# A decoder layer in split fp32: the up projection's weights split by one instruction on each engine, and a table of biases as two products of narrow parts

## The chip, the cores and the metric

The kernel runs on one core of a Trainium2 chip. Its engines have names in the profile: PE multiplies matrices (PEld is its loading of weights), DVE and POOL work elementwise on vectors, ACT does activations, copies and casts, SP issues most loads; every engine takes its own instructions in the order in which they stand in its queue. The metric is the time of one execution on the device, in microseconds (us). The profile is of one such execution.

## The reference

One layer of a hybrid causal decoder on 256 tokens of 1024 features, all in float32. A combined projection feeds three attention mixers (top-64 sparse, dilated windows, blocks); a bias of each head from a table of 32 distance buckets is added to all logits; the mixers' outputs are gated, summed and projected. What follows is the part that the change's larger half lies in:

```python
bias_a = rel_bias[:, :A_HEADS]              # and bias_b, bias_c: columns of one (32, 24) table
logits = jnp.einsum('bqhd,bqkd->bqhk', qb, ksel) * scale + bias_tab[rel_bucket(dist)]
...
x = layer_norm(ALPHA * x + merged @ w_out[i], ln1_g[i], ln1_b[i])
h = jnp.square(jax.nn.relu(x @ w_up[i])) @ w_down[i]
ple = jax.nn.sigmoid(x @ w_ple_gate[i]) * (p[i] @ w_ple[i])
x = layer_norm(ALPHA * x + h + ple, ln2_g[i], ln2_b[i])
```

`w_up` is 1024 x 4096, `w_down` 4096 x 1024.

## The kernel before

**Products of parts.** PE multiplies in the type fp32r, which holds a narrower number than float32. So each operand is split into two parts, hi (the cast of the value) and lo (what the cast lost), and a product is three: hi by hi, hi by lo, lo by hi (`prod`, L183 to L191, matmul in L188). Weights arrive in units of 128 x 1024 or fewer columns (`Weights`, L79 to L139). For a unit, SP issues the load to a raw tile (L102), ACT casts raw to hi (L111, or L109 where the unit lies in an `Apart`), DVE subtracts hi from raw to get lo (L118, or L122 in an `Apart`), and for the first 58 units POOL does a share of the columns. `get` keeps this four units ahead of PE; raw, hi and lo have five buffers each.

**Blocks at listed places.** An `Apart` (L47 to L70) is a tile whose blocks of 128 columns lie at listed offsets. `runs` groups blocks that follow at equal steps; each run takes one instruction of ACT and one of DVE. In the 32 units of the up projection hi has its blocks at 16, 192, 320, ... and lo at 64, 208, 336, ...: the step from the first block to the second is larger than the others, so a run covers blocks 0 and 1 (128 x 256) and another the other six (128 x 768): two instructions on ACT (L109) and two on DVE (L122) per unit.

**The up projection** (L913 to L952). For each unit f, eight matmuls of 512 columns (L923: hi of the unit by both parts of x) and eight of 256 (L926: lo by the hi part of x) go to one PSUM bank. Then DVE adds the two halves (`tensor_reduce`, L907), ACT applies ReLU and square (L908, L909) and casts the result to the hi part of hT (L934), and DVE subtracts for its lo part (L935). Some units come in pairs whose results are combined for the Strassen-like down projection: then POOL forms four sums of the two (L945 to L948) and ACT (L951) and DVE (L952) split all seven blocks at once. Ahead of the down projection, its own operands are formed on DVE (`form`, L885 to L887) from rows of w_down that SP loads to tiles (wr, xr); xr takes the buffer of x1, which L923 and L926 read.

**The table of biases** (`bias_table`, L478 to L488). GpSimd's queue loads a one-hot matrix oh (36 x 384) and relt, the 32 x 24 table with four more rows (two loads, L482 and L483). PE multiplies the two in float32 (L485), ACT copies the 24 x 384 product to tab (L487), stores it to DRAM (L530), and SP reads it back as the tiles T (L265) that the mixers add (L461 and others). It happens between the first features: `feat` multiplies a block of the projection in one of three PSUM banks named mm, which are freed by the ACT cast and DVE subtraction of `k_pair` (L320), `q_pair` (L306, L307) or `v_out` (L400, L401).

**What sets the order.** The source is written once per step; the framework's scheduler lays the instructions of each engine out in a row by estimated times, except where the code pins them (`issue_after`, `keep_in_program_order`). So a change of an instruction's size can move others that it doesn't name.

Of the kernel before, what the change touches and what calls it, by code (L numbers as in the profile page):

```python
# [11 lines left out]
F32 = mybir.dt.float32  # L12
F32R = mybir.dt.float32r
ALU = mybir.AluOpType
# [11 lines left out]
N_BIAS = 24  # L26
# [5 lines left out]
N_U = 384  # L32
# [110 lines left out]
def hybrid_layer(ctx: ExitStack, tc: tile.TileContext, x0, xn, pT, wqk, wva, wvb, wg, wbc, wba,  # L143
                 wout, wup, wdn, wpg, wple, lnrow, rel, onehot, pick, out):
    nc = tc.nc
    pe, act, dve, pool = nc.tensor, nc.scalar, nc.vector, nc.gpsimd
# [55 lines left out]
    def inturn(t):  # L202
        return t.rearrange("p (a c) -> p c a", a=2)
# [28 lines left out]
    def add(*a, at=(0, 0), by=DV):  # L232
        i = n_u[0]
        n_u[0] += 1
        return W.add(*a, by=by if i < 58 else "v", at=at)
# [143 lines left out]
    op = pm.tile([128, 8, 2, S], F32R, name="op")  # L379
# [97 lines left out]

    def bias_table():  # L478
        relt = wk.tile([36, N_BIAS], F32, name="relt", tag="e")
        oh = wk.tile([36, N_U], F32, name="oh", tag="e")  # L480
        pool.dma_start(oh, onehot)
        pool.dma_start(relt[0:N_BUCKETS], rel)  # L482
        pool.dma_start(relt[N_BUCKETS:], pick)  # L483
        tab_ps = next(ps_v)
        pe.matmul(tab_ps[:N_BIAS, :N_U], lhsT=relt, rhs=oh, start=True, stop=True)  # L485
        tab = wk.tile([N_BIAS, N_U], F32, name="tab", tag="e")
        act.copy(tab, tab_ps[:N_BIAS, :N_U])  # L487
        return tab  # L488
# [3 lines left out]
    with ExitStack() as begin:  # L492
# [7 lines left out]
        with tc.high_priority(offset=1000):  # L500
            for k in range(KT):
                for i, (a, b) in enumerate(cut[k]):
                    e = nc.scalar if i else nc.sync
# [9 lines left out]
        for k in range(KT):  # L513
            for i, (w, x) in enumerate(((sh, xh), (sh, xl), (sl, xh))):
                for f in range(FIRST):
                    pe.matmul(pairs(first[f]), lhsT=w[:, k, 128 * f:128 * f + 128],  # L516
                              rhs=inturn(x[:, k]),
                              start=k == i == 0, stop=k == KT - 1 and i == 2)
        iq = [q_pair(ps, 0.125) for ps in first]
    tp, wk, wk2, sm = (right(n, b) for n, b in (("tp", 3), ("wk", 3), ("wk2", 2), ("sm", 6)))  # L520
    tab = bias_table()
    ps = feat(4)
    kI, kA = k_pair(ps[0:64], ps[0:64]), k_pair(ps[64:128], ps[64:128])
# [76 lines left out]
    for j in range(3):  # L600
        s = logits(kA, q)
        o = opair()
        for h in range(2):
# [4 lines left out]
            with tc.issue_after(W.subs[-3]):  # L608
                pool.tensor_tensor(ta[:, 0:128], natural(T, n % 3, 128, 256), am[:, 0:128],
                                   op=ALU.add)  # L610
                pool.tensor_tensor(ta[:, 128:384], natural(T, n % 3, 0, 256), am[:, 128:384],
                                   op=ALU.add)
# [17 lines left out]
    u_out += [add(wout[4 + i], 1024, wo[:, i, 0], wo[:, i, 1]) for i in range(4)]  # L630
    u_ple = [add(wple[i], 1024) for i in range(2)]
    u_pg = [add(wpg[i], 1024) for i in range(8)]
    UP = (16, *range(192, 1088, 128)), (64, *range(208, 1104, 128))
    u_up = [[add(wup[i], 1024, at=UP)] for i in range(32)]

    H = (slice(0, 512), slice(512, 1024))
# [219 lines left out]
    for k in (*SEQ, *LATE):  # L856
        i = PAIRS.index(k) if k in PAIRS else -1
# [39 lines left out]
    for k in (*SEQ, *LATE):  # L897
        if k in PAIRS:
            i = PAIRS.index(k)
# [13 lines left out]
    for f in range(32):  # L913
# [8 lines left out]
        for k, c in enumerate(cs):  # L922
            pe.matmul(ps, lhsT=hi[:, c], rhs=x1[:, :, k].rearrange("p b a t -> p a t b"),  # L923
                      start=k == 0, stop=False)
        for k, c in enumerate(cs):
            pe.matmul(ps[:, 0], lhsT=lo[:, c], rhs=x1[:, :, k, 0].rearrange("p b t -> p t b"),  # L926
                      start=False, stop=k == KT - 1)
# [239 lines left out]
```

## Time and profile before

| what | value |
|---|---|
| median of three runs (lowest, highest) | 417.76 us (416.52, 417.91) |
| the profiled execution | 417.77 us |
| its span, first to last instruction | 416.0 us |
| mean granted TensorE clock | 0.997 |
| PE busy | 405.4 us (97%) |
| DVE busy | 348.6 us (84%) |
| ACT busy | 277.4 us (67%) |
| POOL busy | 121.6 us (29%) |
| HBM read and written | 81.88 and 1.09 MB |

A row of a group of instructions reads: line, engine, operation, output<-inputs, shape and type, xcount | busy us, mean ns of one | idle us of the engine just before them, with what ended most of it. A row of a timeline reads: start, duration (of the whole group if xcount is over 1), engine, line, operation; in brackets the idle time before it and what released it. Durations overlap a little, since an engine starts an instruction before the last one's end is recorded; on PE the spacing of starts is the cost, not the length of one.

### The profile page before, as it was taken

The numbers are of one execution on the slowest core, as the hardware profiler recorded it, in microseconds if no ns is written. First come the engines' busy times: TensorE is split into PE (matmuls) and PEld (weight loads), VectorE is DVE, ScalarE is ACT, GpSimd is POOL, SyncE is SP. The second block draws the span as 40 slices with busy tenths as digits, with TensorE's granted clock in tenths as the row PEclk, the third lists the DMA queues.
The fourth block names the chain that finished last, engine by engine and source line by source line (L and its number), as shares of the span: only waits on it lengthen the run. The fifth ranks groups of instructions, "written<-read, shape, count | busy, mean of one in ns | idle before, by whom it ended". The sixth has DMA issues, their size and how long they took to land.

```text
span 416.0 us, 7828 instructions
## 1 busy us (share of the span) xinstructions
PE 405.4 (97%) x2804; PEld 374.4 (90%) x2804; DVE 348.6 (84%) x650; ACT 277.4 (67%) x530; POOL 121.6 (29%) x128
## 2 busy tenths in 40 slices
PE   8999999999999999999999999999999999999993
PEld 8989999999999999999887889999999988788883
DVE  4968669897777689889968889999999798999856
ACT  6877476495798786867515567887889766467310
POOL 1669456275353657500000002433430000000001
PEclk9999999999999999999999999999999999999998
DMA  8896766567464408478980686786576377556602
GB/s 288 298 327 188 267 165 201 169 201 258 148 204 135 134 9 290 125 218 260 335 310 12 219 284 198 227 288 197 189 215 199 102 277 231 185 167 207 198 2 102
DMA packets 27964, 83.49 MB, mean 201 GB/s; under 512 B 3184, under 2 KB 6792, under 8 KB 27540
## 3 DMA queue, kind: packets, MB, share of 16 engines
q1 hardware_dynamic: 27216, 80.46, 59.9%
q10 hardware_dynamic: 612, 2.46, 1.6%
q8 instruction: 22, 0.36, 0.4%
q14 instruction: 18, 0.15, 0.1%
q0 software_dynamic: 96, 0.06, 0.0%
HBM read 81.88 MB, written 1.09 MB: 199 GB/s over the span
## 4 chain that ended last, share of the span: by engine, by line
PE 82%; DVE 10%; DMA 3%; issue 3%; ACT 1%; POOL 0%; SPq 0%; DVEq 0%; ACTq 0%; POOLq 0%
PE mm L188 36%; PE b L188 16%; PE mm L923 13%; PE mm L926 7%; PE b L370 3%; DMA xr<-in_wdn_dram 3%; DVE wlo L118 3%; PE b L516 3%; PE b L412 1%; DVE wlo L122 1%; PE b L416 1%; ACT whi L111 1%; PE b L179 1%; DVE store L118 1%; DVE G L692 1%
## 5 line engine op out<-in xcount | busy, mean ns | idle before, releaser
L111 ACT CAST whi<-raw 128x1024 fp32r<-128x1024 f32 (+3 forms) x92 | 89.4, 986 | 35.4 <-PE b L188 14.6
L122 DVE TENSOR_TENSOR wlo<-raw,whi 128x256 fp32r<-128x256 f32 (+3 forms) x118 | 94.6, 825 | 16.1 <-ACT whi L111 13.2
L188 PE MATMUL mm<-xh,whi 128*128 128x256 f32 x336 | 89.1, 278 | 0.0
L122 POOL TENSOR_TENSOR wlo<-raw,whi 128x384 fp32r<-128x384 f32 (+1 forms) x50 | 68.6, 1382 | 65.2 <-ACT whi L111 58.6
L188 PE MATMUL mm<-xl,whi 128*128 128x256 f32 x336 | 87.1, 277 | 0.0
L188 PE MATMUL mm<-xh,wlo 128*128 128x256 f32 x336 | 79.4, 278 | 0.0
L188 PEld LDWEIGHTS mm<-xh,whi 128*128 128x128 f32 x336 | 64.4, 192 | 0.9
L188 PEld LDWEIGHTS mm<-xl,whi 128*128 128x128 f32 x336 | 64.5, 192 | 0.3
L923 PE MATMUL mm<-x,whi 128*128 128x512 f32 x256 | 60.7, 379 | 0.0
L188 PEld LDWEIGHTS mm<-xh,wlo 128*128 128x128 f32 x336 | 58.7, 192 | 0.2
L188 PE MATMUL b<-whi,store 128*128 128x512 f32 x168 | 52.6, 380 | 0.7 <-DVE store L698 0.4
L923 PEld LDWEIGHTS mm<-x,whi 128*128 128x128 f32 x256 | 46.1, 190 | 5.2
L118 DVE TENSOR_TENSOR wlo<-raw,whi 128x1024 fp32r<-128x1024 f32 (+2 forms) x38 | 43.3, 1162 | 3.3 <-ACT whi L111 3.1
L740 POOL TENSOR_TENSOR rs<-rs,half 128x1 f32<-128x1 f32 x4 | 2.2, 554 | 143.3 <-DVE rs L739 143.3
L109 ACT CAST whi<-raw 128x256 fp32r<-128x256 f32 x64 | 36.4, 612 | 6.1 <-PE b L188 3.7
L188 PEld LDWEIGHTS b<-whi,store 128*128 128x128 f32 x168 | 31.7, 189 | 5.8 <-DVE store L698 0.8
L926 PEld LDWEIGHTS mm<-x,wlo 128*128 128x128 f32 x256 | 33.6, 191 | 1.7
L926 PE MATMUL mm<-x,wlo 128*128 128x256 f32 x256 | 33.7, 275 | 0.0
L188 PE MATMUL b<-wlo,store 128*128 128x512 f32 x84 | 32.0, 382 | 0.6 <-DVE wlo L118 0.6
L947 POOL TENSOR_TENSOR a<-a 128x128 f32<-128x128 f32 x7 | 7.3, 1044 | 57.3 <-ACT a L909 51.7
L188 PE MATMUL mm<-op,whi 128*128 128x256 f32 x128 | 22.1, 278 | 0.0
L188 PE MATMUL b<-whi,x 128*128 128x512 f32 x64 | 19.8, 384 | 0.1
(223 smaller groups left out, 824.7 us busy)
## 6 DMA issues: line engine op xcount, KB each, us to landing
raw<-in_wup_dram SPq DMA_DIRECT2D x32, 512.0 KB, 4.4
raw<-in_wg_dram SPq DMA_DIRECT2D x24, 512.0 KB, 4.3
raw<-in_wqk_dram SPq DMA_DIRECT2D x18, 512.0 KB, 5.0
raw<-in_wdn_dram SPq DMA_DIRECT2D x18, 512.0 KB, 4.5
raw<-in_wout_dram SPq DMA_DIRECT2D x8, 512.0 KB, 4.6
raw<-in_wpg_dram SPq DMA_DIRECT2D x8, 512.0 KB, 5.9
T<-tabd SPq DMA_DIRECT2D x24, 128.0 KB, 3.9
xr<-in_wdn_dram SPq DMA_DIRECT2D x6, 512.0 KB, 3.6
```

The source lines that it names most:

```text
L109: i = nc.scalar.copy(blocks(hi, a, b), blocks(r, a, b))
L111: i = nc.scalar.copy(hi, r)
L118: i = e.tensor_tensor(lo[:, x], r[:, x], hi[:, x].bitcast(F32), op=ALU.subtract)
L122: i = e.tensor_tensor(blocks(lo, *x), blocks(r, *x), blocks(hi, *x).bitcast(F32), op=ALU.subtract)
L179: pe.transpose(t[:, 0:128], ident, ident)
L188: i = pe.matmul(ps, lhsT=a[x], rhs=b[y], start=first and n == 0, stop=last and n == 2, skip_group_check=more)
L370: m = pe.matmul(ss[2 * n + h][:, QC[b]], lhsT=q[d, x, c], rhs=k[d, y, 0:128 * (b + 1)], start=i == 0, stop=i == 2)
L412: pe.transpose(t[:, 128 * i:128 * i + 128], P[:, 128 * i:128 * i + 128], ident)
L516: pe.matmul(pairs(first[f]), lhsT=w[:, k, 128 * f:128 * f + 128], rhs=inturn(x[:, k]), start=k == i == 0, stop=k == KT - 1 and i == 2)
L923: pe.matmul(ps, lhsT=hi[:, c], rhs=x1[:, :, k].rearrange("p b a t -> p a t b"), start=k == 0, stop=False)
L926: pe.matmul(ps[:, 0], lhsT=lo[:, c], rhs=x1[:, :, k, 0].rearrange("p b t -> p t b"), start=False, stop=k == KT - 1)
L947: pool.tensor_tensor(sums[2], a11, a21, op=ALU.subtract)
```

## The change

The offsets of the up units become 64 (hi) and 80 (lo), single numbers: hi and lo of such a unit are then plain slices, and the split is one cast (L111) and one subtraction (L118) of 128 x 1024.

In `bias_table`, relt is split into two fp32r parts of 36 x 24 by a copy on ACT (L485 of the changed kernel) and a subtraction on DVE (L486); oh becomes fp32r, so its load converts; and PE multiplies oh by each part, both into the same bank (L489). Four tiles take turns in the buffers of tag "e" where three did. Lines behind this place have numbers greater by four in the changed kernel: L530 becomes L534, L907 L911, L935 L939, L952 L956.

```diff
     def bias_table():
         relt = wk.tile([36, N_BIAS], F32, name="relt", tag="e")
-        oh = wk.tile([36, N_U], F32, name="oh", tag="e")
+        parts = wk.tile([36, 2, N_BIAS], F32R, name="parts", tag="e")
+        oh = wk.tile([36, N_U], F32R, name="oh", tag="e")
         pool.dma_start(oh, onehot)
         pool.dma_start(relt[0:N_BUCKETS], rel)
         pool.dma_start(relt[N_BUCKETS:], pick)
+        act.copy(parts[:, 0], relt)
+        dve.tensor_tensor(parts[:, 1], relt, parts[:, 0].bitcast(F32), op=ALU.subtract)
         tab_ps = next(ps_v)
-        pe.matmul(tab_ps[:N_BIAS, :N_U], lhsT=relt, rhs=oh, start=True, stop=True)
+        for i in range(2):
+            pe.matmul(tab_ps[:N_BIAS, :N_U], lhsT=parts[:, i], rhs=oh, start=i == 0, stop=i == 1)
         tab = wk.tile([N_BIAS, N_U], F32, name="tab", tag="e")
         act.copy(tab, tab_ps[:N_BIAS, :N_U])
         return tab
...
-    UP = (16, *range(192, 1088, 128)), (64, *range(208, 1104, 128))
+    UP = 64, 80
     u_up = [[add(wup[i], 1024, at=UP)] for i in range(32)]
```

The order of instructions moves at more places than the diff names. On ACT, near the start, where k is the split of a key's feature, parts the split of relt, and ri the scores of the top-64 selection (difference from before):

```order
 L320 CAST k<-mm 64x256
+L485 CAST parts<-relt 36x24
 L111 CAST whi<-raw 128x1024
 L320 CAST k<-mm 64x256
-L538 ACTIVATE ri<-b_463 128x384
-L538 ACTIVATE ri<-b_462 128x384
-L538 ACTIVATE ri<-b_465 128x384
-L538 ACTIVATE ri<-b_464 128x384
-L487 COPY tab<-b_309 24x384
+L542 ACTIVATE ri<-b_467 128x384
```

The cast of relt stands ahead of the cast of a unit of weights and of the fourth cast of k; before, nothing stood between the third L320 and that L111. Further down the same row, the store of the table:

```order
 L400 CAST V<-mm 128x5x64
 L399 COPY iw<-mm 128x8
-L530 DMA tabd<-tab 24x384
 L400 CAST V<-mm 128x5x64
-L542 ACTIVATE ri<-ri,iw 128x128 x4
-L111 CAST whi<-raw 128x1024
```
```order
+L111 CAST whi<-raw 128x1024
+L534 DMA tabd<-tab 24x384
+L546 ACTIVATE ri<-ri,iw 128x128 x4
```

The store stood between the two casts of V; it now stands behind both and behind a cast of weights. On DVE, late in the up projection, where a_4176 is the pair of units 20 and 21, q_4239 unit 22 and a_4270 unit 23; before:

```order
L907 TENSOR_REDUCE a_4176<-mm 128x256 x2
L122 TENSOR_TENSOR wlo<-raw,whi 128x2x128
L122 TENSOR_TENSOR wlo<-raw,whi 128x768
L907 TENSOR_REDUCE q_4239<-mm 128x256
L122 TENSOR_TENSOR wlo<-raw,whi 128x2x128
L122 TENSOR_TENSOR wlo<-raw,whi 128x768
L935 TENSOR_TENSOR store<-q_4239,store 128x256
L907 TENSOR_REDUCE a_4270<-mm 128x256
L122 TENSOR_TENSOR wlo<-raw,whi 128x2x128
L122 TENSOR_TENSOR wlo<-raw,whi 128x768
L952 TENSOR_TENSOR store<-a_4176,store 128x896
```

And in the changed kernel, where the same pair is a_4130, unit 22 q_4189 and unit 23 a_4218:

```order
L911 TENSOR_REDUCE a_4130<-mm 128x256
L118 TENSOR_TENSOR wlo<-raw,whi 128x1024
L911 TENSOR_REDUCE q_4189<-mm 128x256
L118 TENSOR_TENSOR wlo<-raw,whi 128x1024
L956 TENSOR_TENSOR store<-a_4130,store 128x896
L911 TENSOR_REDUCE a_4218<-mm 128x256
L118 TENSOR_TENSOR wlo<-raw,whi 128x1024
L939 TENSOR_TENSOR store<-q_4189,store 128x256
```

The subtraction of the pair stood behind the reduction of unit 23 and now stands ahead of it.

## The prediction

> **What bounds the kernel now.** I read the page first, then busy time by stage, then the chain of waits, then the timelines of the two places that the change touches.
>
> ```profile
> span 416.0 us, 7828 instructions
> ...
> PE 405.4 (97%) x2804; PEld 374.4 (90%) x2804; DVE 348.6 (84%) x650; ACT 277.4 (67%) x530; POOL 121.6 (29%) x128
> ```
>
> The execution took 417.77 us, of which 1.77 lie around the span of 416.0; the median of the runs shown is 417.76, so sums against this execution can be taken as sums against the median. PE is idle for 10.6 us in all. The next view gives two stages, the up projection and the start of the down projection: length, then busy us (and count) of PE, PEld, DVE, ACT, POOL.
>
> ```profile
> 239.80:328.30 88.50, 88.50 (x535) 81.09 (x534) 83.44 (x131) 73.01 (x154) 21.48 (x28) 1.00 0.66 209
> 328.30:362.00 33.70, 33.01 (x151) 27.87 (x150) 30.24 (x33) 20.82 (x25) 0.00 (x0) 1.00 0.71 234
> ```
>
> In the up stage PE is busy for all of 88.50 us at full clock. DVE is nearly as full, but PE never waits for it. In the next 33.70 us PE idles 0.69. The chain of waits says how the two are joined:
>
> ```profile
> 325.68 1.73 PE mm L923 x8
> 327.41 0.90 PE mm L926 x8
> 329.18 4.38 DMA xr<-in_wdn_dram
> ...
> 334.73 1.23 DVE wlo L118
> ...
> 361.49 2.64 PE b L188 x11
> ```
>
> The last up unit ends at 328.31; that releases the load of xr (it takes the place of x1, which those products read), and from there a chain of DMA, ACT and DVE steps runs to 361.49, where PE has waited for it. What lengthens that chain lengthens the kernel; what shortens the up units' casts shortens nothing that PE waits for.
>
> **One instruction for a unit's split.** The groups of instructions, shapes kept apart (busy us, mean ns):
>
> ```profile
> L111 ACT CAST whi<-raw 128x1024 fp32r<-128x1024 f32 x72 | 74.2, 1046 | 32.9 <-PE b L188 14.6 <-PE mm L188 7.5 <-issue 4.5
> L118 DVE TENSOR_TENSOR wlo<-raw,whi 128x1024 fp32r<-128x1024 f32 x30 | 36.0, 1220 | 3.3 <-ACT whi L111 3.1
> L122 DVE TENSOR_TENSOR wlo<-raw,whi 128x768 fp32r<-128x768 f32 x36 | 35.7, 992 | 1.6 <-ACT whi L111 1.1 <-ACT whi L109 0.5
> L109 ACT CAST whi<-raw 128x768 fp32r<-128x768 f32 x32 | 26.5, 829 | 0.0
> L122 DVE TENSOR_TENSOR wlo<-raw,whi 128x256 fp32r<-128x256 f32 x32 | 14.0, 439 | 1.3 <-ACT whi L109 1.3
> L109 ACT CAST whi<-raw 128x256 fp32r<-128x256 f32 x32 | 12.7, 396 | 6.1 <-PE b L188 3.7 <-PE mm L923 2.3
> ```
>
> ACT pays 396 + 829 = 1225 ns per unit and would pay 1046, DVE 439 + 992 = 1431 and would pay 1220: 179 and 211 ns less, over 32 units 5.7 us of ACT and 6.8 us of DVE. I count both at nothing: what hides them is the 88.50 us of PE without a gap. There is no cover to lose here, since the work shrinks.
>
> What can cost is the new order. On DVE the sum part of a pair (units 20 and 21, L952) stood behind the reduction of unit 23; now it stands ahead of it. Line L952 needs ACT's L951, which needs POOL's sums of the pair, and everything behind it on DVE waits too: unit 23's reduction first, then its square on ACT and all later units.
>
> ```profile
> 302.10 1.73 PE mm L923 x8
> 303.66 1.28 DVE L907 TENSOR_REDUCE a<-mm 128x256 f32<-128x512 f32 x2
> 306.54 0.42 ACT L909 ACTIVATE a<-a 128x256 f32<-128x256 f32 x1
> 309.48 0.95 ACT L951 CAST store<-a 128x896 fp32r<-128x896 f32 x1 [0.29 <-POOL a L948]
> 310.52 1.08 DVE L952 TENSOR_TENSOR store<-a,store 128x896 fp32r<-128x896 f32 x1
> 320.93 0.68 DVE L907 TENSOR_REDUCE q<-mm 128x256 f32<-128x512 f32 x1
> 323.33 0.68 DVE L907 TENSOR_REDUCE a<-mm 128x256 f32<-128x512 f32 x1
> 328.34 0.69 DVE L907 TENSOR_REDUCE a<-mm 128x256 f32<-128x512 f32 x1
> 332.04 0.42 DVE L935 TENSOR_TENSOR store<-a,store 128x256 fp32r<-128x256 f32 x1
> 333.05 1.22 DVE L885 TENSOR_TENSOR rows<-xr 128x1024 f32<-128x1024 f32 x1 [0.59 <-DMA xr<-in_wdn_dram]
> ```
>
> Unit 21's products end at 302.10 (unit 22 begins then); its reduction is the second of the pair of 1.28 us, from about 304.3 to 304.94: it lags PE by 2.2 us. From its end to the end of L952, 311.60, are 6.66 us. Of these the square waits until 306.54 behind two casts of weights that the new order doesn't put there; with reduction, two activations of 0.42 and no cast between, some 1.1 us go, and 5.55 are left. Unit 23's reduction would then begin 5.55 + 0.64 = 6.2 us after unit 21's, where PE needs 2 x 2.62 = 5.24 for two units: its lag is 0.95 greater than unit 21's, up to 3.1. Behind it a unit takes 2.40 us on DVE and ACT (320.93 to 323.33), 0.22 less than PE's 2.62, so in the eight units to the last the lag falls by 1.8: to 1.35, or to 0 if the lighter DVE has worked unit 21's lag off before. In the profile of before it is 0.03 there (328.34 against 328.31).
>
> How much of that reaches PE? With no lag, L935 ends at 332.46, L885 waits for xr until 333.05, ends at 334.27, and the next link starts at 334.73. So 334.73 - 332.46 - 1.22 = 1.05 us of lag are free. What remains is 1.35 - 1.05 = 0.3 at the one end, 0 at the other; since PE already waits at 361.49, what remains would be added to the time in full. I take **+0.2**, with 0 and 0.8 as ends (0.8: unit 21 half a microsecond later than now).
>
> **The table.** The timelines around it, and the load of the last piece of relt:
>
> ```profile
> 27.62 0.82 PE L485 MATMUL b<-oh,relt 36*24 36x384 f32 x2
> 28.37 0.41 PE L188 MATMUL mm<-whi,xl 128*128 128x328 f32 x1
> 29.03 0.27 PE L188 MATMUL mm<-xh,wlo 128*128 128x256 f32 x1
> ...
> 24.90 0.37 ACT L320 CAST k<-mm 64x256 fp32r<-64x256 f32 x1
> 25.70 1.05 ACT L111 CAST whi<-raw 128x1024 fp32r<-128x1024 f32 x1 [0.42 <-DMA raw<-in_wqk_dram]
> 29.23 0.16 ACT L399 COPY iw<-mm 128x8 f32<-128x8 f32 x1
> ...
> 26.78 0.83 DVE L122 TENSOR_TENSOR wlo<-raw,whi 128x640 fp32r<-128x640 f32 x1 [0.49 <-ACT whi L111]
> 27.64 0.43 DVE L320 TENSOR_TENSOR k<-mm,k 64x256 fp32r<-64x256 f32 x1
> ...
> 21.20 0.52 POOL L483 DMA_DIRECT2D relt<-in_pick_dram  x1
> ```
> ```profile
> relt<-in_pick_dram POOLq DMA_DIRECT2D x1, 0.4 KB, 5.6
> ```
>
> On PE the fp32 product takes 28.37 - 27.62 = 0.75 us. A product of 256 columns takes 0.90/8 = 0.112 us and one of 512 takes 1.73/8 = 0.216, so two of 384 should take 2 x 0.164 = 0.33: 0.35 less, leaving a little for the change of rows. [...]
>
> The new cast of relt stands on ACT behind the third L320 and ahead of L111, and ACT takes its instructions in order. Relt is whole when its last load lands: 21.20 + 5.6 = 26.8. ACT had gone on to L111 at 25.70. Now: cast from 26.8 to 26.96 (0.16, as the small copy L399), L111 until 28.01, DVE's L122 from 28.04, its L320 0.86 later (27.64 - 26.78), from 28.90 to 29.33. PE waits for exactly that: mm has three banks, two hold the value products, and the products of the next feature (29.03) need the bank that this last L320 reads. PE would arrive at 29.03 - 0.35 = 28.68 and start at about 29.4. The net is 29.4 - 29.03 = **+0.4**, whatever the table product itself has gained: the 0.35 vanish in the wait. Ends: -0.35, if relt lands early enough or the wait isn't there; +1.0, if ACT's lateness meets the next place as well, where slack is small. DVE's subtraction of relt (24 elements) falls into time in which DVE waits for L111 anyway.
>
> The store of the table to DRAM moves on ACT's queue behind the two V casts and an L111, and with it the T loads on SP:
>
> ```profile
> 29.36 0.56 ACTq L530 DMA_DIRECT2D tabd<-tab  x1
> 33.72 3.18 SPq L265 DMA_DIRECT2D T<-tabd  x7
> 47.52 0.29 DVE L461 CUSTOM_DVE_ANT_0 eb<-b,T 128x128 f32<-128x128 f32 x1 [1.28 <-PE b L370]
> ```
>
> L111 adds about 1 us and the lateness above 1.3: T loads some 2.5 to 3.5 us later, with 47.52 - (33.72 + 3.18) = 10.6 us between the last issue of the seven and the first use. I count nothing; one load of weights, which now passes three of the T loads on SP, gains a little.
>
> **Sum:** 417.77 + 0.4 + 0.2 = 418.4 us.
>
> **The rivals.** What this kernel's measurement can tell from no change is about 0.3%, or 1.25 us: faster means under 416.5, slower over 419.0.
>
> *Nothing but the product's gain* (chance 0.22): relt lands 0.7 us earlier or the bank is free, and the lag stays under 1.05. 417.77 - 0.35 = 417.4. For it: both waits are thin; against: 5.6 us is what this very load took.
>
> *The relief arrives* (0.10): the down projection's chain starts with less queued on ACT and DVE, and PE's 0.69 us of idling there go too. 417.4 - 0.7 = 416.7, and lower if later gaps shrink with it. Against: the chain begins with a load that only the last product of the up stage releases, and in that stage PE has no gap.
>
> *The layout* (0.12), which ends slower. Block 0 of hi and of lo moves from an offset of its own (16, 64) to one in line with the others (64, 80). Each is loaded as weights while the products of the other half stream, so 2 x 32 = 64 loads change their relation to the stream. Two groups of the same shape:
>
> ```profile
> L923 PE MATMUL mm<-x,whi 128*128 128x512 f32 x256 | 60.7, 379 | 0.0
> L416 PE MATMUL b<-pt,V 128*128 128x512 f32 x16 | 6.5, 405 | 0.0
> ```
>
> L416 is 26 ns slower at the same size, so the place of operands, or who else uses them, can matter. 64 x 26 ns = 1.7 us on a stage where PE is the bound: 418.4 + 1.7 = 420.1. It decides from about 10 ns per load on. Against it: that L416's 26 ns come from addresses is not shown. [...]
>
> *The loads on GpSimd's queue* (0.11): oh is now converted on its way, and if it or what is queued behind it lands 1 us later, each of these goes to PE one for one: 419.4.
>
> My forecast has 0.45. With its terms' ends it lies between 417.4 and 419.6, about three in ten of it over 419.0. **Slower** is 0.45 x 0.3 + 0.11 (layout) + 0.08 (loads) = 0.33, **faster** 0.06 of the relief and 0.04 of all else, **same** the rest, 0.57. The range of 417.0 to 420.2 takes in all but the relief and the far ends of the last two rivals.
>
> **What would show it.** Right: ACT's cast of relt at 26.8 behind some 1.5 us of idling, PE waiting about 0.7 us ahead of the products at 29.4, both up groups still 379 and 275 ns, unit 23's reduction 2 to 3 us behind PE and the last at most 1.5, the end of the up stage about 0.4 later than before, and L885 at or just behind the landing of xr. Wrong: an up stage longer than 88.5 us (layout), relt's cast later than 27.5 (loads), no wait ahead of the feature's products, or the link at 361.49 coming earlier against the end of the up stage (relief).

## The result, and the profile after

The changed kernel took 421.32 us (median of 11 runs, 419.06 to 424.10) where the kernel before took 417.58 (11 runs, 416.52 to 419.17): a ratio of 1.008 (95% interval 1.0058 to 1.0103), 3.7 us slower. The forecast was 418.4 with a range of 417.0 to 420.2; it was wrong. Two later measurements of the same changed kernel gave 1.0077 (1.006 to 1.0094) and 1.0057 (1.0039 to 1.0076).

The profiled execution of the changed kernel is the fastest of its 11: 419.06 us, with a span of 416.9, so 2.16 lie around the span where 1.77 did. First its page, busy time, then the up projection and the start of the down projection by the same columns as before.

```profile
span 416.9 us, 7778 instructions
...
PE 405.0 (97%) x2804; PEld 374.5 (90%) x2804; DVE 346.0 (83%) x619; ACT 274.8 (66%) x499; POOL 120.3 (29%) x128
```
```profile
241.32:329.81 88.49, 88.49 (x536) 81.05 (x534) 79.52 (x99) 69.45 (x123) 20.64 (x28) 1.00 0.66 208
329.81:362.65 32.84, 32.28 (x150) 27.81 (x148) 30.21 (x34) 22.01 (x27) 0.00 (x0) 1.00 0.71 239
```

The up stage lost 3.9 us of DVE's work and 3.6 of ACT's, and is as long as it was: 88.49 us, PE busy for all of it. The down projection's start is not longer either. So the loss lies ahead of 241. There, around the table's product (lines of PE, then ACT, then DVE; in brackets idle time and its releaser):

```profile
27.02 0.56 PE L489 MATMUL b<-oh,parts 36*24 36x384 f32 x2
27.50 0.41 PE L188 MATMUL mm<-whi,xl 128*128 128x328 f32 x1
...
28.02 0.30 PE L188 MATMUL mm<-whi,xl 128*128 128x328 f32 x1
29.37 0.35 PE L188 MATMUL mm<-xh,wlo 128*128 128x256 f32 x1 [1.04 <-DVE k L320]
```
```profile
24.93 0.37 ACT L320 CAST k<-mm 64x256 fp32r<-64x256 f32 x1
26.74 0.21 ACT L485 CAST parts<-relt 36x24 fp32r<-36x24 f32 x1 [1.44 <-DMA relt<-in_pick_dram]
26.86 1.04 ACT L111 CAST whi<-raw 128x1024 fp32r<-128x1024 f32 x1
...
26.99 0.18 DVE L486 TENSOR_TENSOR parts<-relt,parts 36x24 fp32r<-36x24 f32 x1 [0.68 <-ACT parts L485]
27.94 0.83 DVE L122 TENSOR_TENSOR wlo<-raw,whi 128x640 fp32r<-128x640 f32 x1 [0.77 <-ACT whi L111]
28.80 0.43 DVE L320 TENSOR_TENSOR k<-mm,k 64x256 fp32r<-64x256 f32 x1
```

This is the forecast wait, at the forecast place: the cast at 26.74 (26.8 was said), the feature's products at 29.37 (29.4). A little later PE's row differs in a way that the forecast doesn't have. Before, the 24 products of the logits stood in one piece:

```profile
30.46 1.65 PE L370 MATMUL b<-k,q 64*128 64x128 f32 x24
32.04 0.38 PE L188 MATMUL mm<-xh,whi 128*128 128x256 f32 x1
32.25 0.28 PE L188 MATMUL mm<-xl,whi 128*128 128x256 f32 x1
```

Now one product of a feature (256 columns of 128 rows) stands between the first of them and the other 23:

```profile
30.88 0.32 PE L370 MATMUL b<-k,q 64*128 64x128 f32 x1
31.13 0.38 PE L188 MATMUL mm<-xh,whi 128*128 128x256 f32 x1
31.44 1.64 PE L370 MATMUL b<-k,q 64*128 64x128 f32 x23
33.00 0.38 PE L188 MATMUL mm<-xl,whi 128*128 128x256 f32 x1
```

The 24 logits and that one product take 33.00 - 30.88 = 2.12 us; before, where the product stood behind them (32.04) and the next began at 32.25, they took 32.25 - 30.46 = 1.79: 0.33 more for the same work. Then a third place. ACT, POOL and PE of the changed kernel, and ACT and POOL of the kernel before:

```profile
34.87 0.87 ACT L542 ACTIVATE ri<-b 128x384 f32<-128x384 f32 x2 [1.72 <-POOL idx L547]
...
37.92 0.39 ACT L320 CAST k<-mm 128x256 fp32r<-128x256 f32 x1
...
32.06 1.18 POOL L122 TENSOR_TENSOR wlo<-raw,whi 128x384 fp32r<-128x384 f32 x1 [2.44 <-ACT whi L111]
33.21 4.34 POOL L547 TENSOR_TENSOR idx<-idx,ri 128x128 f32<-128x128 f32 x6
...
40.28 0.35 PE L188 MATMUL mm<-xh,wlo 128*128 128x256 f32 x1 [0.42 <-DVE k L320]
```
```profile
36.01 0.38 ACT L320 CAST k<-mm 128x256 fp32r<-128x256 f32 x1
...
30.77 2.26 POOL L543 TENSOR_TENSOR idx<-idx,ri 128x128 f32<-128x128 f32 x4 [2.31 <-ACT ri L542]
32.99 1.59 POOL L122 TENSOR_TENSOR wlo<-raw,whi 128x384 fp32r<-128x384 f32 x1
```

Since the cast of weights L111 moved ahead of ACT's scores of the selection (L546), POOL gets its share of those weights first and its sums idx later; ACT waits 1.72 us for them, its L320 comes 1.9 us later (37.92 against 36.01), and the next feature's products wait for that.

The three places can be measured in every profile by the starts of PE's products: from the table's product to the first logits product ("first stretch": 30.46 - 27.62 = 2.84 before, 30.88 - 27.02 = 3.86 after), the logits with that one product (1.79 and 2.12), and from there the next 87 products ("third stretch": 9.72 and 10.48), 130 in all from the table's product. The sum is 14.35 us before and 16.46 after: 2.11 more. The time from there to the end of the span is 374.02 before and 373.44 after (374.26 and 374.52 in the profiles of e1 and e12, the same changed kernel). These are the columns of the table further down.

### The profile page after: what moved, and what is told of

Read it like the earlier page. It is cut to its first block, busy times and chain, and to the rows that moved or that the text cites. A ratio compares the mean times of both kernels' runs of the same rounds, so it can differ in the third digit from the quotient of the medians.

```text
span 416.9 us, 7778 instructions
## 1 busy us (share of the span) xinstructions
PE 405.0 (97%) x2804; PEld 374.5 (90%) x2804; DVE 346.0 (83%) x619; ACT 274.8 (66%) x499; POOL 120.3 (29%) x128
## 4 chain that ended last, share of the span: by engine, by line
PE 79%; DVE 11%; issue 3%; ACT 2%; DMA 2%; POOL 0%; SPq 0%; DVEq 0%; ACTq 0%; POOLq 0%
PE mm L188 34%; PE b L188 16%; PE mm L927 13%; PE mm L930 7%; DVE wlo L118 4%; PE b L370 3%; PE b L520 3%; DMA xr<-in_wdn_dram 2%; PE b L412 1%; ACT whi L111 1%; DVE wlo L122 1%; PE b L416 1%; DVE store L118 1%; PE b L179 1%; DVE G L696 1%
## 5 line engine op out<-in xcount | busy, mean ns | idle before, releaser
L111 ACT CAST whi<-raw 128x1024 fp32r<-128x1024 f32 (+3 forms) x124 | 122.5, 1000 | 39.4 <-PE b L188 18.2
L118 DVE TENSOR_TENSOR wlo<-raw,whi 128x1024 fp32r<-128x1024 f32 (+2 forms) x70 | 82.3, 1189 | 5.8 <-ACT whi L111 5.5
L122 POOL TENSOR_TENSOR wlo<-raw,whi 128x384 fp32r<-128x384 f32 (+1 forms) x50 | 66.7, 1345 | 69.5 <-ACT whi L111 62.3
L122 DVE TENSOR_TENSOR wlo<-raw,whi 128x640 fp32r<-128x640 f32 (+2 forms) x54 | 53.3, 995 | 13.8 <-ACT whi L111 12.9
L930 PEld LDWEIGHTS mm<-x,wlo 128*128 128x128 f32 x256 | 33.6, 191 | 1.7
L951 POOL TENSOR_TENSOR a<-a 128x128 f32<-128x128 f32 x7 | 3.9, 561 | 54.5 <-ACT a L913 54.5
L188 PEld LDWEIGHTS mm<-op,whi 128*128 128x128 f32 x128 | 18.8, 192 | 0.3
```

Of the source, the lines that this page charges most:

```text
L111: i = nc.scalar.copy(hi, r)
L118: i = e.tensor_tensor(lo[:, x], r[:, x], hi[:, x].bitcast(F32), op=ALU.subtract)
L122: i = e.tensor_tensor(blocks(lo, *x), blocks(r, *x), blocks(hi, *x).bitcast(F32), op=ALU.subtract)
L188: i = pe.matmul(ps, lhsT=a[x], rhs=b[y], start=first and n == 0, stop=last and n == 2, skip_group_check=more)
```

## The experiments

Theories, by the letters that stand in the expectations: **A**, the cost comes from ACT's queue standing behind the load of relt; **B**, it is the waits of single executions, which vary; **C**, it comes from the up projection; **D**, the two narrow products or the converting load of oh cost by themselves. After the first runs, **E**: three places, the wait for relt, the feature's product between the logits, and ACT waiting for POOL, add up; against it **F**: the product between the logits is hidden, and **G**: the wait near 39 comes from ACT's casts and not from POOL's order. **H**: the loss of TensorE's clock that some executions show has nothing to do with the wait at 29.

**e1_again**: the changed kernel once more, unedited.

> The changed kernel once more, for its spread and for one more profile. Its profiled execution of before this run took 419.06 us with a mean clock of 0.995, others took up to 424.10 with 0.984. Theory A (the executions differ in a loss of granted clock at one place, the rest of the program is the same): the times lie again between 419 and 424, spans grow by about 0.4 us for each 0.001 of mean clock that is lost, and if this profile has caught a mean clock under 0.993, the TensorE clock falls under 1.0 in one stretch of a few us. Rival B (the waits themselves vary from execution to execution): times scatter at the same mean clock.

Measured 420.86 (6 runs, 419.94 to 421.93), ratio 1.0077 (1.006 to 1.0094); PE's three stretches 3.87, 2.13 and 10.47. They repeat to 0.02 us, so these waits don't change from one profile to the other, which speaks against B. All six executions kept a clock of 0.994 or more and still spread over 2.0 us; the link of time and clock that A expected can't be seen here, and where this spread comes from stays open.

**e2_up_only**: the kernel before, with the up projection's half alone.

```diff
-    UP = (16, *range(192, 1088, 128)), (64, *range(208, 1104, 128))
+    UP = 64, 80
```

> Only the offsets of the up units change (64 and 80), the table stays one float32 product. Theory A, the cost comes from the table's wait near 29 us: this kernel takes the time of the kernel before within 0.5 us (417.3 to 418.3 median) and shows no loss of clock. Rival C, the cost comes from the up projection (the subtraction of the pair ahead of the next reduction, or the layout): 418.5 to 421, with the last reduction of the up stage 1 to 3 us behind PE.

Measured 417.79 (12 runs, 417.39 to 418.88), ratio 1.0002 (0.9989 to 1.0015). This half moves nothing, so C falls, and with it the layout rival.

**e3_table_only**: the kernel before, with the table's half alone (the diff of `bias_table`).

> Only the table changes, the up units keep their two runs. Theory A: the whole of the cost, 420 to 421.5 median, with the wait of about 1.0 us ahead of the products at 29.4 and a mean clock under 0.993 in some executions. Rival C: 417.8 to 418.5, only the wait's own 0.4 us.

Measured 419.86 (7 runs, 418.98 to 422.42), ratio 1.0055 (1.0034 to 1.0076). The stretches are those of the whole change: 3.87, 2.13, 10.48. The loss at the three places is the table's. The changed kernel's medians lie 0.4 to 1.7 us further above the kernel before than this one; that is taken up below, at the span and at the clock.

**e4_dve_cast**: the changed kernel with relt's cast on DVE.

```diff
-        act.copy(parts[:, 0], relt)
+        dve.tensor_copy(parts[:, 0], relt)
```

> The changed kernel with one instruction moved: relt's hi part is cast by DVE instead of ACT, so ACT's casts of weights and of k no longer stand behind the load of relt. Both halves of the change stay. Theory A: the wait ahead of the products at 29.4 goes, PE gains the product's 0.3 us, and the median falls to 417.3 to 418.3, with no executions over 420. Rival C: only some 0.7 us are gained on the changed kernel, 420 to 421. Rival B: the scatter stays as wide as 5 us.

Measured 421.88 (5 runs, 420.75 to 422.33), ratio 1.0094 (1.0076 to 1.0111): no help. On DVE the cast holds up what stands behind it as it did on ACT:

```profile
28.34 0.17 DVE L485 CAST parts<-relt 36x24 fp32r<-36x24 f32 x1 [2.94 <-DMA relt<-in_pick_dram]
28.55 0.17 DVE L486 TENSOR_TENSOR parts<-relt,parts 36x24 fp32r<-36x24 f32 x1
28.64 0.81 DVE L122 TENSOR_TENSOR wlo<-raw,whi 128x640 fp32r<-128x640 f32 x1
29.49 0.43 DVE L320 TENSOR_TENSOR k<-mm,k 64x256 fp32r<-64x256 f32 x1
```

The step that needs relt stands in DVE's row ahead of steps that don't, as it stood in ACT's, and A's forecast for this run (417.3 to 418.3) failed. How much a cast on DVE would cost with relt on time isn't shown: in this profile the last load was issued at 22.01 and landed 6.2 us later, at 28.2, where it landed at 26.7 in the changed kernel, so the cast came 1.6 us later.

**e5_early_relt**: the changed kernel, with relt loaded at the start on ACT's queue and split among the first casts, so that nothing waits for it at 27.

```diff
+    relt = keep.tile([36, N_BIAS], F32, name="relt")
+    parts = keep.tile([36, 2, N_BIAS], F32R, name="parts")
...
+            act.dma_start(relt[0:N_BUCKETS], rel)
+            act.dma_start(relt[N_BUCKETS:], pick)
...
+        act.copy(parts[:, 0], relt)
+        dve.tensor_tensor(parts[:, 1], relt, parts[:, 0].bitcast(F32), op=ALU.subtract)
         iq = [q_pair(ps, 0.125) for ps in first]
```

> The changed kernel with relt loaded at the start by ACT's queue into a buffer of its own and split there, among the first casts; both halves of the change and the two narrow products stay, and so does the new order on PE that puts one product of 256 columns between the first and the second product of the second set of logits. Theory A (the loss starts with ACT's queue standing behind the load of relt): the 1.0 us wait ahead of the feature at 29.4 goes and the 0.5 us wait at the feature near 38.8 too; what stays is about 0.4 us for the product put between the logits, against 0.3 us of gain in the table's product: 417.5 to 418.3. Rival D (the two products or the converting load of oh cost by themselves): 419.5 to 421.

Measured 418.97 (12 runs, 417.74 to 419.62), ratio 1.0024 (1.0011 to 1.0038). PE around the product:

```profile
27.37 0.51 PE L485 MATMUL b<-oh,parts 36*24 36x384 f32 x2
27.81 0.41 PE L190 MATMUL mm<-whi,xl 128*128 128x328 f32 x1
...
28.47 0.27 PE L190 MATMUL mm<-xh,wlo 128*128 128x256 f32 x1
```

The wait is gone and the product's own gain appears: 27.81 - 27.37 = 0.44 us where float32 took 0.75, 0.31 less (0.35 was estimated). The logits still take 2.13 and the third stretch 10.37: two of three places are left. A had expected the wait near 39 to go with the one at 29; it stayed, and is E's third place.

**e6_wait_only**: the kernel before, with relt split on ACT and DVE into parts that nothing uses; the float32 product stays.

```diff
+        parts = wk.tile([36, 2, N_BIAS], F32R, name="parts", tag="e")
+        act.copy(parts[:, 0], relt)
+        dve.tensor_tensor(parts[:, 1], relt, parts[:, 0].bitcast(F32), op=ALU.subtract)
```

> The kernel before, with the split of relt on ACT and DVE added and its result not used: the table stays one float32 product of relt and oh, oh's load does not convert, the up units keep their two runs. Theory A: this alone costs 1.5 to 2.5 us, 419.2 to 420.4, with a wait of 0.7 to 1.1 us ahead of the feature at 29.4. Rival D: 417.5 to 418.3, since products and load of oh are those of before.

Measured 419.4 (12 runs, 417.75 to 419.93), ratio 1.0027 (1.0012 to 1.0042). The wait without the products costs time too, and ends where it ended in the changed kernel:

```profile
27.56 0.82 PE L488 MATMUL b<-oh,relt 36*24 36x384 f32 x2
...
29.55 0.35 PE L188 MATMUL mm<-xh,wlo 128*128 128x256 f32 x1 [0.42 <-DVE k L320]
```

The logits take 1.79 here. ACT's order behind the table is that of the kernel before, and yet the third stretch is 10.21: so ACT's lateness from relt by itself can make 0.49 of the 0.76 us that the third stretch grew by (ACT's L320 comes at 37.14, 1.13 us later than before, but PE's logits, at 31.05, only 0.59).

**e7_oh_only**: the kernel before, with oh converted on its load to fp32r and read as float32 (`oh.bitcast(F32)`) by the old product.

> The kernel before, with one thing changed: oh is an fp32r tile, so that its load converts, and is read as float32 by the same single product. The order of the instructions is that of before. Theory A: no difference, 417.4 to 418.3, oh lands within 1 us of what it did. Rival D, for the converting load: relt lands at least 1 us later and PE waits ahead of the table's product, 418.5 or more.

Measured 417.69 (12 runs, 416.82 to 418.42), ratio 0.9995 (0.9981 to 1.0008). The converting load costs nothing; D falls on this side, and on the other by e5.

**e8_late_relt**: the changed kernel with two idle loads of relt's size between its two loads (their data is used by nothing), to land the second later.

```diff
+        for n in range(2):
+            with tc.issue_after(i.ins):
+                i = pool.dma_start(keep.tile([N_BUCKETS, N_BIAS], F32, name=f"more{n}"), rel)
+        with tc.issue_after(i.ins):
+            pool.dma_start(relt[N_BUCKETS:], pick)
```

> The changed kernel with two small loads that nobody reads put on GpSimd's queue between the two loads of relt, so that its last piece lands about 1.05 us later (two issues of about 0.53). Theory A: one for one, 1.0 to 1.3 us on the changed kernel's 420.9, so 421.8 to 422.8, with the wait ahead of the feature near 2 us; and if it is an idle stretch of PE that makes the clock fall in some executions, more of them have a mean clock under 0.993 than of the changed kernel (6 of 17). Rival D: less than 0.4 us more.

Measured 421.13 (6 runs, 420.57 to 421.68), ratio 1.0074 (1.0055 to 1.0093): less than expected. Relt's last load landed at 22.60 + 4.7 = 27.3, only 0.6 us later than in the changed kernel, where 1.05 was intended. The profiled execution waits ahead of the table's product instead (1.07 us, by a subtraction of DVE that took 3.43 us), so it doesn't tell the theories apart.

**e9_no_between**: e5, with the second half of that feature's products held behind the logits.

```diff
+                if wait is not None and k >= 4:
+                    behind.enter_context(tc.issue_after(wait))
```

> The kernel of the early load of relt, with one thing more: the second half of the feature's products is told to stand behind the second set of logits, so that no product stands between the first and the second of these. ACT, POOL and DVE keep the changed kernel's order. Theory E (the table's half costs in three places: the wait for relt, the product between the logits, and ACT waiting for POOL near 34): the logits take 1.8 us again instead of 2.13, about 0.4 us less than the kernel of the early load (418.97), 418.3 to 418.8; the wait near 39 stays. Rival F (the product between the logits is hidden, since the second product of the logits would have waited for a bank anyway): no gain, 418.8 to 419.2, and a wait ahead of the second product of the logits.

Measured 418.42 (12 runs, 417.64 to 420.64), ratio 1.0018 (1.0004 to 1.0032). The logits are back at 1.78, with no wait among them. The median doesn't settle the product's price: the interval overlaps that of e5. The profiled execution (420.64) is the slowest of the twelve, so its whole says little; PE reaches the table early, at 26.51, and waits 0.18 us ahead of the feature for DVE's L327, and its third stretch is 10.60, with ACT and POOL in the changed kernel's order, though nothing waited for relt.

**e10_neither**: e9, with the copy of the table on DVE, which leaves ACT and POOL behind the logits in the order of the kernel before.

```diff
-        act.copy(tab, tab_ps[:N_BIAS, :N_U])
+        dve.tensor_copy(tab, tab_ps[:N_BIAS, :N_U])
```

> As the last, and the copy of the finished table goes to DVE instead of ACT; by this POOL takes its four sums of the scores ahead of the next unit's subtraction again, as in the kernel before. Theory E: the 0.6 us wait near 39 goes as well, and all that is left is the table's gain of 0.3 us and what lies around the span: 417.3 to 418.1. Rival G (the wait near 39 comes from the casts and scores that moved on ACT, not from POOL's order): it stays, 418.3 to 418.8.

Measured **417.09** (12 runs, 415.91 to 418.16), ratio **0.9981 (0.997 to 0.9992)**: below both kernels, though by less than the 0.3% that was set as the bound. All three places are gone:

```profile
27.45 0.51 PE L491 MATMUL b<-oh,parts 36*24 36x384 f32 x2
...
28.55 0.27 PE L190 MATMUL mm<-xh,wlo 128*128 128x256 f32 x1
...
29.98 1.64 PE L377 MATMUL b<-k,q 64*128 64x128 f32 x24
```

What is left of the change is the product's gain, 0.32 us over the three stretches. Between F and E the rows decide for E: in e9 and e10 the 24 logits stand in a row and nothing waits in place of the product that stood there. The intervals of e5 and e10 lie apart, so that the second and third place together cost time is shown by the medians too. G isn't excluded: e6 has the wait with the old order, e9 has it with the new order and without lateness. Either one makes it.

**e11_later3** and **e12_after_look**: the changed kernel with three idle loads of 32 x 2 (unused) ahead of relt's last, and a third measurement of the changed kernel beside it.

```diff
+        for n in range(3):
+            with tc.issue_after(i.ins):
+                i = pool.dma_start(keep.tile([N_BUCKETS, 2], F32, name=f"more{n}"), rel[:, 0:2])
```

> The changed kernel with three small loads that nobody reads ahead of relt's last piece, about 1.5 us more until it lands. Theory A with the clock: PE's wait ahead of the feature grows towards 2.5 us, the time by 1.2 to 1.8 us where the clock is whole (422 to 422.8), and half of the executions or more have a mean clock under 0.993; if this profile catches one, the granted clock falls to 0.5 within some 5 us behind that wait. Rival H (the loss of clock has nothing to do with the wait): no more executions with a loss than the changed kernel had, 6 of 17, or the fall lies elsewhere.

> The changed kernel a third time, beside the others on this chip. Theory A: 420.5 to 421.5 median; two or three of these executions have a mean clock under 0.993 and are 1 to 4 us longer than those with a whole clock.

e11: 421.9 (6 runs, 420.64 to 423.88), ratio 1.0103 (1.0075 to 1.0131); e12: 420.22 (5 runs, 419.92 to 420.86), ratio 1.0057 (1.0039 to 1.0076). In e11's profile PE waits 0.99 us ahead of the table's product and again 1.04 ahead of the feature. Three of e11's six executions lost clock (0.986 to 0.990), none of e12's, so the medians' difference of 1.7 us holds two things. The three of e11 that kept their clock took 420.64 to 420.99, 0.7 us more than e12 at the middle one, and relt's last load landed 0.7 us later (22.81 + 4.9 = 27.7 against 21.26 + 5.7 = 27.0): what depends on relt passes its lateness on. Two expectations failed: 422 to 422.8 for e11 with a whole clock, and two or three executions of e12 with a loss of clock.

**e13_clock_look** and **e14_clock_look2**: the kernel of e11, each run once, for a profile of an execution that loses clock. Runs list a mean granted clock of 0.994 to 0.998 for most executions, but 0.984 to 0.991 for some of the changed kernel's.

> The changed kernel with three small loads ahead of relt's last piece, once more, for a profile of an execution that lost clock (half of them did). If the mean clock is under 0.993: theory A, the granted clock falls to 0.5 for some 3 to 7 us at a place between 27 and 36 us, behind PE's waits, and the products there take twice their spacing; rival H, it falls at another place, such as the start or the stage from 380 on. If the clock is whole, the span is 418.5 to 419 and the look tells nothing.

> The same look a second time, with the same expectations: with a clock under 0.993, theory A puts its fall between 27 and 36 us, rival H elsewhere; with a whole clock the span is 418.5 to 419.

e13 took 421.18 with a clock of 0.998 and so tells nothing on this. e14 took 422.59 with 0.990. Its busy time by stretches of 2 us (the column behind POOL's is the granted clock), then PE:

```profile
28.00:30.00 2.00, 1.14 (x6) 0.67 (x5) 1.22 (x2) 1.95 (x5) 1.20 (x1) 1.00 0.79 252
30.00:32.00 2.00, 1.82 (x8) 1.85 (x9) 0.53 (x3) 2.00 (x9) 0.43 (x1) 0.53 0.71 266
32.00:34.00 2.00, 2.00 (x12) 1.54 (x12) 2.00 (x4) 1.96 (x5) 1.13 (x1) 0.61 0.69 230
34.00:36.00 2.00, 2.00 (x28) 1.86 (x27) 1.89 (x3) 0.33 (x1) 1.84 (x4) 1.00 0.06 18
```
```profile
27.82 0.56 PE L493 MATMUL b<-oh,parts 36*24 36x384 f32 x2 [0.51 <-ACT parts L489]
...
28.83 0.30 PE L188 MATMUL mm<-whi,xl 128*128 128x328 f32 x1
30.18 0.55 PE L188 MATMUL mm<-xh,wlo 128*128 128x256 f32 x1 [1.05 <-DVE k L320]
30.53 0.42 PE L188 MATMUL mm<-xh,whi 128*128 128x256 f32 x1
30.75 0.42 PE L188 MATMUL mm<-xl,whi 128*128 128x256 f32 x1
```

The clock is full to the end of the wait and half right behind it: the same products start 0.22 us apart that start 0.11 apart elsewhere. The trace's record of the granted clock has it at 0.5 from 30.14 to 33.55 us, and full from 33.55 to 415.84. So the loss lies right behind the wait, where A put it, and H's place for it falls for this execution. That the wait is its cause is argued from the place and from the counts below.

**e15_longer**: the changed kernel with six idle loads, and with the next cast of weights pinned behind relt's cast, for a longer wait.

```diff
+        for n in range(6):
+            with tc.issue_after(i.ins):
+                i = pool.dma_start(keep.tile([N_BUCKETS, 2], F32, name=f"more{n}"), rel[:, 0:2])
...
+        W.behind[8] = (act.copy(parts[:, 0], relt).ins,)
```

> The changed kernel with six small loads ahead of relt's last piece, about 3 us more until it lands, and the cast of the next unit's weights told to stand behind relt's on ACT. The scheduler now puts the fourth cast of k ahead of it and the table's products later on PE. Theory A: PE waits 2 us or more around 29 to 33, the time is 422.5 to 426, most executions have a mean clock under 0.993, and the fall lies behind this wait. Rival H: clock whole in most executions although PE waits as long.

Measured 422.2 (9 runs, 419.45 to 423.67), ratio 1.01 (1.0069 to 1.0131). The wait didn't grow: the scheduler put value and feature products between the two products of the table, and PE waits 1.04 us, now for the second part. So it is no test of length. But its nine runs fall in two: four of 419.45 to 420.04 with a clock of 0.995 or more, five of 422.20 to 423.67 with 0.987 to 0.989.

All kernels side by side: the three stretches of PE and their sum against the kernel before, from the profiled executions, and the difference of the medians. A wait ahead of the table's product is not in the stretches: 0.43 us in e1, 0.72 in e4, 1.07 in e8, 0.99 in e11. In e15 PE's products have another order, so its stretches hold as many products as the others' but not the same ones.

| kernel | first | logits | third | sum - 14.35 | median - before |
|---|---|---|---|---|---|
| e2 up half | 2.85 | 1.79 | 9.71 | 0.00 | -0.1 |
| e7 oh converted | 2.84 | 1.79 | 9.72 | 0.00 | -0.1 |
| changed | 3.86 | 2.12 | 10.48 | 2.11 | 3.7 |
| e1 changed | 3.87 | 2.13 | 10.47 | 2.12 | 3.0 |
| e12 changed | 3.77 | 2.12 | 10.48 | 2.02 | 2.4 |
| e3 table half | 3.87 | 2.13 | 10.48 | 2.13 | 2.0 |
| e4 cast on DVE | 4.18 | 2.13 | 10.65 | 2.61 | 4.0 |
| e8 two idle loads | 3.12 | 2.13 | 10.47 | 1.37 | 3.4 |
| e11 three idle loads | 3.87 | 2.13 | 10.47 | 2.12 | 4.1 |
| e15 six, pinned | 4.02 | 2.05 | 9.72 | 1.44 | 4.6 |
| e6 split, unused | 3.49 | 1.79 | 10.21 | 1.14 | 1.7 |
| e5 relt early | 2.53 | 2.13 | 10.37 | 0.68 | 1.2 |
| e9 and logits whole | 2.96 | 1.78 | 10.60 | 0.99 | 0.6 |
| e10 and old order | 2.53 | 1.79 | 9.71 | -0.32 | -0.7 |

## Why the prediction was wrong

**What failed is the table's term**, "The net is 29.4 - 29.03 = +0.4", with +1.0 as its upper end. The rows of three engines behind the table had changed (the front part of this document shows the cast L111 ahead of ACT's scores), and only the place of the first wait was priced. By the runs the table costs 2.1 us at three places:

- the wait at 29: 0.94 us from the table's product to the feature (2.35 against 1.41), and 0.08 in the next stretch. The forecast's arithmetic held to 0.03 us: cast at 26.74, end of the wait at 29.37. But it was set against an execution that reached the table at 27.62, later than the others (27.25 and 27.29 in e7 and e2; 27.02 to 27.41 in the changed kernel's). The end of the wait is tied to relt's landing, so an earlier PE only waits longer; 0.4 was too little by about half a microsecond.
- the product between the logits: 0.33 us, and 0.10 behind. No term, no rival. It is in PE's new order, which the forecast read only around the table.
- the wait near 40: 0.65 us by the starts of the products (0.42 in the row's bracket, which counts idle time alone). The text has it only in an upper end ("if ACT's lateness meets the next place as well, where slack is small"). It should have been in the sum: that slack could have been read from the rows of before, where DVE's L320 ends at 38.58 and the products that wait for it start at 38.84.

**Then there are 0.35 us around the span**, by the traces' spans to the nanosecond: 2.12 to 2.17 in the profiled executions of the changed kernel (e1 and e12 too), e5, e8, e9, e11 and e13 to e15, but 1.78 to 1.79 in those of the kernel before, e2, e3, e4, e6, e7 and e10. 2.1 + 0.35 = 2.5, and the six runs of the first measurement that kept their clock (0.995 or more) have a median of 420.0, 2.5 above the kernel before; e3, without the 0.35, is 2.0 above it, with 2.13 in its stretches. The forecast had no term for this. The cause stays open: e10 differs from e9 only in the copy of the table, and e4 from the changed kernel only in relt's cast. One number goes with it: the ten profiles with the longer time count 499 instructions of ACT, the other seven 498, 530 or 531. What that does outside the span, no run shows.

**And then the clock.** The other five runs of that measurement have a clock of 0.984 to 0.991 and took 421.37 to 424.10 (median 421.77, 1.7 more than the six; 3.41 us at half clock, as e14 shows them, would lose PE 1.7, an estimate). Over all measurements, 19 of 57 executions of the kernels whose profile shows a wait of about 1 us or more at this place (the changed kernel, e3, e4, e8, e11 to e15) had a clock below 0.993, and none of 154 of the others (the kernel before where its clock is on record, e2, e5, e6, e7, e9, e10). One profile, e14's, shows the loss right behind the wait; that the wait causes it, there and in the rest, is argued from the place and these counts. Against a plain rule, e1 and e12, the same changed kernel, lost none in 11. The forecast had no such case.

Point by point, the rest:

- **Up projection at nothing**: right. The up groups keep their 379 and 275 ns (below) and the stage its 88.5 us; e2 is 1.0002. The casts and subtractions saved less than the 5.7 and 6.8 us that were worked out, 3.6 and 3.9 in the stage: the means that were added overlap a little.

```profile
L927 PE MATMUL mm<-x,whi 128*128 128x512 f32 x256 | 60.6, 379 | 0.0
...
L930 PE MATMUL mm<-x,wlo 128*128 128x256 f32 x256 | 33.7, 275 | 0.0
```

- **The layout rival** (1.7 us): nothing. These two rows have 379 and 275 ns as before, and e2 is 1.0002.
- **Lag at the end of the up stage** (+0.2): the mechanism came as described, the cost didn't. DVE, and the load of xr:

```profile
305.93 0.68 DVE L911 TENSOR_REDUCE a<-mm 128x256 f32<-128x512 f32 x1
...
311.10 1.09 DVE L956 TENSOR_TENSOR store<-a,store 128x896 fp32r<-128x896 f32 x1 [1.32 <-ACT store L955]
312.11 0.68 DVE L911 TENSOR_REDUCE a<-mm 128x256 f32<-128x512 f32 x1
...
330.82 0.68 DVE L911 TENSOR_REDUCE a<-mm 128x256 f32<-128x512 f32 x1
...
334.85 1.22 DVE L889 TENSOR_TENSOR rows<-xr 128x1024 f32<-128x1024 f32 x1
```
```profile
330.63 4.37 DMA xr<-in_wdn_dram
362.33 2.64 PE b L188 x11
```

  Unit 21's reduction to unit 23's are 6.18 us (6.2 was said); PE ends unit 23 eight units of 2.62 before 329.77, at 308.8, so it lags by 3.3 (up to 3.1 was said), and the last unit by 330.82 - 329.77 = 1.05, which is the slack that was worked out as free. From the end of the last up product to the link it is 362.33 - 329.77 = 32.56 us in this profile and 33.3 and 33.6 in e1's and e12's, against 33.18 before: no cost to be seen, and no relief, since PE still idles 0.56 us in this stretch (0.69 before).
- **Loads on GpSimd's queue**: nothing; relt's last load took 5.4 us from issue to landing, against 5.6, and e7 is 0.9995.
- **The T loads**: right at nothing. The first is issued at 34.02 (33.72 before), 0.3 us later and not 2.5 to 3.5 as was said, and the first use at 49.03 waits for PE.
- **The product's gain**: 0.31 against 0.35, and, as said, hidden in the wait; e5 and e10 show it. In e5 the 0.75 us of float32 became 0.44.

## What to carry to other kernels

A new step that needs a late load stands in a row with steps that don't: look up when the load lands, and issue it early enough, or place the step behind the others, before moving work between engines for it. When a scheduler lays out the rows, compare the rows of all engines from the edited place to the next fixed one, and price each moved block there; here two of three costs lay outside the lines that were edited. Expect that a stall of PE may cost more than its length: here the executions with a loss of clock were all of kernels that wait about 1 us or more (19 of their 57, and none of 154 of the others), though the link is argued.

## What the runs showed of the hardware that was not expected

**In e14, waits of 0.51 and 1.05 us were followed by 3.41 us at half clock.** The clock stays at 0.5 for 3.413 us; the stretches at full clock that the trace has on record ahead of that and behind it are 23.893 and 382.293 us, 7 and 112 times 3.4133. In the profiles of the kernel before and of the changed kernel the one such stretch is 406.186 us in both, 119 times 3.4133. What sets these lengths, no run shows.

In the 3.41 us ahead of e14's loss, 26.72 to 30.14, PE was idle for 1.52 us (the two waits; the last 0.04 of the second lie behind the 3.41). Near the ends of two spans the clock fell behind more idle time: at 413.87 us in the profile of the kernel before, with PE idle for all of the 3.41 us ahead, and at 412.82 in the changed kernel's, with PE idle for 2.86 of them. e13, the same kernel as e14, waited 0.6 and 1.0 us at the same two places and has a mean clock of 0.998. Why some executions of one kernel lose clock and others don't was not shown.

**One product put between others of another shape cost PE 0.33 us.** The one between the logits is 128*128 among 64*128: it starts 31.13 - 30.88 = 0.25 behind the first logits product, and the other 23 start 0.31 behind it, where products of its size in a row start 0.11 apart, and the logits' 1.65/24 = 0.07. That the shape is the reason was not tried by itself.
